# 48 gathered tokens in place of 64, one gathered row every 5.75 ticks, and four smaller edits around them

## The chip, the cores and the metric

The kernel runs on one core of one Trainium2 chip. The metric is the device time of one execution in microseconds (us). A profile of one execution goes with it: the span of the program, every instruction of the engines PE (matmul, with PEld for its weight loads), DVE, ACT, POOL and SP, the DMA queues, and the clock granted to PE.

## The reference

One decoder layer on 256 tokens of width 2048, in float32. Two token mixers are computed and merged (stage 1 below); the part that the change touches is the retrieval layer behind them. Each token has 8 heads; a head scores 128 + 128 keys, keeps 16 of each half and then the best 16 of their 256 sums, so that a token chooses 128 out of 16384 experts. An expert is one row of `expert_u` and one row of `expert_v`, 2048 numbers each.

```
q = h @ w_q                                   # 256 x 2048, 8 heads x 2 halves x 128
s1, s2 = q_half . sub_keys                    # 128 scores each
t1, i1 = top_k(s1, 16); t2, i2 = top_k(s2, 16)
ts, ti = top_k(t1[:, None] + t2[None, :], 16) # idx = i1 * 128 + i2
gate = softmax(ts)
act  = gelu(einsum('td,ted->te', h, expert_u[idx]))
y    = einsum('te,ted->td', gate * act, expert_v[idx])
out  = RMSNorm(x + y)
```

## The kernel before, in words

Everything is emitted in one program order; each engine runs its own instructions in that order, and waits for others by semaphores. Tokens lie along the free axis, so a weight block of 128 x 128 is the stationary operand and the tokens are the moving columns. For precision every weight block is split into a high part (ACT, `hi`, line 95) and a low part (DVE, `lo`, line 97), and the product uses high x (high and low tokens) and low x high tokens.

1. *Mixers* (to about 486 us of the profiled span).
2. *Queries* (about 486 to 585 us): 16 blocks of `w_q`; `query` scales each by the token's RMS factor `rstd2`; `scores` multiplies with the keys; the top-16 searches of tokens 128 to 255 run on DVE as side work (`topk_head`, `finish_topk(1)`). Those of tokens 0 to 127 are kept for stage 4.
3. *Dense loop* (about 585 to 1253 us): 128 steps, one for each block of 128 experts. `run_u` multiplies the block of `expert_u` with the first ND = 192 tokens: per step 16 pairs of matmuls, a wide one of 2 x ND = 384 columns (lines 796 and 800) and a narrow one of ND = 192 columns (lines 797 and 799), each with its own load of 128 x 128 weights. `evac` adds the two halves and stores the scores to a scratch array in DRAM, four blocks at a time (line 818). The last NG = 64 tokens are not in these matmuls: beside the loop, `u_job` gathers their chosen rows of `expert_u` (a gather fetches 128 rows of 8 KB, 1.05 MB) and DVE multiplies them with the token (line 674). A gather holds 8 experts of 16 tokens, so there are NG = 64 gathers, in groups of 16; `token_rows` makes for each group a tile `h2n` with the 16 tokens' vectors repeated in 8 partition blocks: PE transposes, ACT copies, and 7 copies from SBUF to SBUF on SP's DMA queue (line 750), the queue of the weights (`raw`). `v_job` gathers the 128 rows of `expert_v` of one token and multiplies them on PE (line 692, 8 matmul records). Gathers of both kinds go through `step`, with ROWS = 5 buffers. `work` is called four times a step; each call is a tick, and every PACE = 4.5 ticks `step` consumes one gathered row tile and issues a new gather on POOL.
4. *Tail* (from about 1253 us): the other `v_job`s, with one gather of elements (`se`, line 847) each: for one dense token, its 128 scores out of the scratch array. 16 elements make a group, `coefs` turns them into coefficients (DVE, ACT, DVE). `finish_topk(0)` comes here too: PE transposes of its result stand in PE's order (lines 630 and 631) between two `v_job`s.

`rest` are the gather jobs that the dense loop has not issued; the elements of the first group are spread over them.

Of the kernel before, what the change touches and what calls it, by code (L numbers as in the profile page):

```python
# [8 lines left out]
F32 = mybir.dt.float32  # L9
F32R = mybir.dt.float32r  # L10
F16 = mybir.dt.float16
U32 = mybir.dt.uint32
# [22 lines left out]
GT = 16  # L35
NG = 64
ND = T - NG
# [3 lines left out]
ROWS = 5  # L41
PACE = 4.5
FIRST_PACE = 6
LAST_PACE = 3
LEAD = 3
# [67 lines left out]
def block_kernel(ctx: ExitStack, tc: tile.TileContext,  # L113
# [9 lines left out]

    s_dram = nc.dram_tensor("s_scratch", (NK * P, ND), F32, kind="Internal").ap()

# [380 lines left out]
    idxS = gs.tile([P, ND], U32, name="idxS")  # L506
    gT = gs.tile([P, T], F32, name="gT")
    tpos = gs.tile([P, ND], F32, name="tpos")
    ident = gs.tile([P, P], F32, name="ident")
# [14 lines left out]
    run_b(ps, hhl, KC, whole=True)  # L524
    mean_square(accq, rstd2)
    mrg_stack.close()
    mix_stack.close()
# [73 lines left out]
    def finish_topk(tb):  # L601
# [12 lines left out]
        nd = min(ND, (tb + 1) * P) - tb * P  # L614
        if tb == TB - 1:
            pt = bank()
            for g in range(NG // GT):
# [16 lines left out]
        V.tensor_copy(idxV[:, ts], pt[:, 0:P])  # L634
        V.scalar_tensor_tensor(idxS[:, tb * P:tb * P + nd], pt[:, 0:nd], float(ND), tpos[:, tb * P:tb * P + nd],
                               op0=ALU.mult, op1=ALU.add)
# [97 lines left out]
    def token_rows(groups):  # L734

        for g in groups:
# [10 lines left out]

            def copies(g=g):
                for r in range(1, REP):
                    nc.sync.dma_start(h2n[g][r * GT:(r + 1) * GT], h2n[g][0:GT])  # L750

            later(copies, 2)

# [4 lines left out]
    def scores(n, qt):  # L758
# [5 lines left out]
        for tb in range(TB):  # L764
            S.copy(sc[tb], sp[:, tb * P:(tb + 1) * P])
        sc_keep[n] = sc
# [5 lines left out]
    def query(ps):  # L772
        qt = tkt.tile([P, T], F32, name="qt")
        V.tensor_mul(qt, ps[:, :T], rstd2)
        return qt
# [29 lines left out]
    def evac(i, ps):  # L805
# [11 lines left out]
        def store():  # L817
            nc.sync.dma_start(s_dram[(i + 1 - KB) * P:(i + 1) * P].rearrange("(k j) t -> j k t", j=P), es)

# [3 lines left out]
    for i in range(NK):  # L823
        if i == NK - 2:
            clock[2] = LAST_PACE
        ps = bank()
        run_u(ps)
        if i == 0:
            scores(15, qt)
            side.append(finish_topk(1))  # L830
        later(lambda i=i, ps=ps: evac(i, ps))
# [33 lines left out]
    left = GT  # L865
    for k, job in enumerate(rest):
        n = -(-left // (len(rest) - k)) if k >= 2 * len(rest) - GT else 1
        n = min(n, left)
# [72 lines left out]
```

## Time and profile before

| | us |
|---|---|
| median of 3 runs | 1833.71 (1832.51 to 1834.63) |
| the profiled execution | 1830.82 |
| its span | 1829.1 |
| busy in the span: PE / DVE / ACT / POOL | 1593.8 / 1062.4 / 727.0 / 594.0 |

The profiled execution's time is 1.7 us over its span and 2.9 us (0.16%) under the median. PE's busy time contains its pipeline latency, so how full PE is must be read from the starts of its matmuls, not from this sum.

### The profile page before, as it was taken

The numbers are of one execution on the slowest core, as the hardware profiler recorded it, in microseconds if no ns is written. First come the engines' busy times: TensorE is split into PE (matmuls) and PEld (weight loads), VectorE is DVE, ScalarE is ACT, GpSimd is POOL, SyncE is SP. The second block draws the span as 40 slices with busy tenths as digits, with TensorE's granted clock in tenths as the row PEclk, the third lists the DMA queues.
The fourth block names the chain that finished last, engine by engine and source line by source line (L and its number), as shares of the span: only waits on it lengthen the run. The fifth ranks groups of instructions, "written<-read, shape, count | busy, mean of one in ns | idle before, by whom it ended". The sixth has DMA issues, their size and how long they took to land.

```text
span 1829.1 us, 28362 instructions
## 1 busy us (share of the span) xinstructions
PE 1593.8 (87%) x10406; PEld 1190.9 (65%) x10406; DVE 1062.4 (58%) x2143; ACT 727.0 (40%) x1404; POOL 594.0 (32%) x607
## 2 busy tenths in 40 slices
PE   9999999999999899999999999997656666666665
PEld 7978888888899899899989999994111111111111
DVE  7887777777699789778767787776650000000000
ACT  7545555555544455555555555552010000000010
POOL 0130000000155311111112111113757777776762
PEclk9999999999999999999999999997767667667666
DMA  8546666566648799999999999998989999999997
GB/s 323 171 160 186 193 185 186 191 188 186 201 157 202 284 406 403 355 399 415 413 361 407 414 411 412 400 415 304 406 352 404 410 410 410 409 410 409 406 411 323
DMA packets 140012, 598.39 MB, mean 327 GB/s; under 512 B 21345, under 2 KB 37729, under 8 KB 98337
## 3 DMA queue, kind: packets, MB, share of 16 engines
q0 software_dynamic: 52496, 336.99, 45.9%
q1 hardware_dynamic: 87376, 259.60, 40.7%
q8 instruction: 81, 1.33, 0.3%
q14 instruction: 59, 0.48, 0.1%
HBM read 578.16 MB, written 14.68 MB: 324 GB/s over the span
## 4 chain that ended last, share of the span: by engine, by line
PE 41%; issue 30%; DMA 13%; POOL 11%; DVE 4%; SPq 0%; ACT 0%; POOLq 0%; DVEq 0%; ACTq 0%
PE acc L796 19%; DMA rows<-in_exp_v,idxV 9%; PE acc L797 8%; POOL rows L647 6%; POOL se L847 5%; PE y L692 3%; DMA raw<-in_exp_u 3%; PE acc L247 2%; PE acc L245 2%; PE acc L246 2%; DVE lo L97 1%; PE acc L800 1%; PE acc L251 1%; PE acc L252 1%; PE acc L250 1%
## 5 line engine op out<-in xcount | busy, mean ns | idle before, releaser
L97 DVE TENSOR_TENSOR lo<-raw,hi 128x512 fp32r<-128x512 f32 x854 | 577.3, 706 | 215.3 <-ACT hi L95 210.4
L95 ACT CAST hi<-raw 128x512 fp32r<-128x512 f32 x904 | 542.2, 619 | 357.7 <-PE acc L796 147.3
L796 PE MATMUL acc<-hhl,hi 128*128 128x384 f32 x1920 | 570.0, 364 | 5.7 <-ACT hi L95 5.7
L692 PE MATMUL y<-rows,cd 128*32 128x512 f32 x2048 | 380.2, 830 | 195.3 <-DMA rows<-in_exp_v,idxV 193.7
L797 PE MATMUL acc<-hhl,lo 128*128 128x192 f32 x1920 | 485.2, 253 | 3.8 <-DVE lo L97 3.7
L796 PEld LDWEIGHTS acc<-hhl,hi 128*128 128x128 f32 x1920 | 364.6, 190 | 38.7 <-ACT hi L95 28.0
L797 PEld LDWEIGHTS acc<-hhl,lo 128*128 128x128 f32 x1920 | 369.9, 193 | 6.5 <-DVE lo L97 6.5
L647 POOL DMA_INDIRECT rows<-in_exp_v,idxV x256 | 247.9, 968 | 359.7 <-DVE rows L674 228.5
L692 PEld LDWEIGHTS y<-rows,cd 128*32 128x32 f32 x2048 | 47.6, 125 | 474.3 <-DMA rows<-in_exp_v,idxV 431.8
L259 PE MATMUL acc<-hhl,hi 128*128 128x512 f32 x640 | 227.4, 398 | 1.6 <-ACT hi L95 1.6
L656 DVE TENSOR_TENSOR cx<-se,rstd 128x16 f32<-128x16 f32 x12 | 2.1, 175 | 363.6 <-DMA se<-s_scratch,idxS 363.6
L847 POOL DMA_INDIRECT se<-s_scratch,idxS x192 | 183.7, 957 | 70.1 <-issue 58.0
L261 PE MATMUL acc<-hhl,lo 128*128 128x256 f32 x600 | 169.3, 282 | 1.1 <-DVE lo L97 1.1
L657 ACT ACTIVATE cx<-cx 128x16 f32<-128x16 f32 x16 | 3.5, 216 | 407.5 <-DVE cx L656 407.5
L647 POOL DMA_INDIRECT rows<-in_exp_rows,idxU x64 | 68.9, 1077 | 267.0 <-DVE rows L674 195.8
L674 DVE SCALAR_TENSOR_TENSOR rows<-rows,h2n 128x2048 f32<-128x2048 f32 x64 | 146.1, 2283 | 0.0
L259 PEld LDWEIGHTS acc<-hhl,hi 128*128 128x128 f32 x640 | 119.7, 189 | 26.7 <-ACT hi L95 2.0
L541 POOL DMA_DIRECT2D keys<-in_keysT x1 | 0.6, 566 | 371.8 <-PE acc L305 371.8
L261 PEld LDWEIGHTS acc<-hhl,lo 128*128 128x128 f32 x600 | 114.0, 190 | 4.3 <-DVE lo L97 2.8
L245 PE MATMUL acc<-hhl,hi 128*128 128x256 f32 x384 | 110.3, 287 | 0.0
L247 PE MATMUL acc<-hhl,lo 128*128 128x256 f32 x384 | 109.0, 284 | 1.3 <-DVE lo L97 1.3
L246 PE MATMUL acc<-hhl,hi 128*128 128x256 f32 x384 | 108.6, 283 | 0.0
(191 smaller groups left out, 1738.3 us busy)
## 6 DMA issues: line engine op xcount, KB each, us to landing
raw<-in_exp_u SPq DMA_DIRECT2D x256, 512.0 KB, 9.7
raw<-in_w_in SPq DMA_DIRECT2D x96, 512.0 KB, 3.6
raw<-in_w_out SPq DMA_DIRECT2D x32, 512.0 KB, 4.0
raw<-in_w_q SPq DMA_DIRECT2D x32, 512.0 KB, 3.9
s_scratch<-es SPq DMA_DIRECT2D x32, 384.0 KB, 11.6
raw<-in_w_gproj SPq DMA_DIRECT2D x16, 512.0 KB, 4.6
raw<-in_w_v SPq DMA_DIRECT2D x15, 512.0 KB, 7.5
rows<-in_exp_v,idxV POOLq DMA_INDIRECT x256
```

The lines of the kernel that those rows point to most:

```text
L95: self.nc.scalar.copy(h, t)
L97: eng.tensor_sub(l, t, h.bitcast(F32))
L245: nc.tensor.matmul(ps, whi, ahi, start=first, stop=False)
L247: nc.tensor.matmul(ps, wlo, ahi, start=False, stop=last)
L259: nc.tensor.matmul(ps, whi, both, start=first, stop=last)
L261: nc.tensor.matmul(ps[:, :T], wlo, act[:, 0], start=False, stop=False)
L647: nc.gpsimd.indirect_dma_start(out=r, out_offset=None, in_=src, in_offset=bass.IndirectOffsetOnAxis(ap=idx, axis=0))
L674: V.scalar_tensor_tensor(r, r, 1.0, h2n[g], op0=ALU.mult, op1=ALU.mult, accum_out=act[g][:, n:n + 1])
L692: nc.tensor.matmul(y[q * GQ:(q + 1) * GQ], cd[:, m * GQ:(m + 1) * GQ], r[:, q * 512:(q + 1) * 512], start=(m == 0), stop=(m == GT - 1))
L796: nc.tensor.matmul(o2, whi[:, w], hhl[:, k, :, 0:ND], start=(k == 0), stop=False)
L797: nc.tensor.matmul(o1, wlo[:, w], hhl[:, k, 0, 0:ND], start=False, stop=False)
L847: nc.gpsimd.indirect_dma_start(out=se[t0][:, m:m + 1], out_offset=None, in_=flat, in_offset=bass.IndirectOffsetOnAxis(ap=idxS[:, t0 + m:t0 ...
```

## The change

NG goes from 64 to 48, so ND from 192 to 208: the dense matmuls have 416 and 208 columns, there are 48 gathers of `expert_u` in 3 groups, and 208 element gathers. The pace goes to 5.75 ticks and, for the last three steps, 2.5. The scratch array puts the four blocks of a store side by side, so a partition writes one piece of 3328 bytes where it wrote four of 768, and `finish_topk` computes the other index. The 7 copies of a token group are issued one at a time, some ticks apart. The query goes from PSUM to SBUF by an ACT copy without the factor, the factor is applied when the scores are copied, and for this the factor is brought into partitions (`rs2`) by two small matmuls. `finish_topk(1)` has 3.0 us of side-work credit more ahead of its matmuls.

```diff
--- before.py
+++ after.py
@@ -33,15 +33,15 @@
 AHEAD = 4
 WARM = 10
 GT = 16
-NG = 64
+NG = 48
 ND = T - NG
 REP = P // GT
 GQ = 32
 NQ = P // GQ
 ROWS = 5
-PACE = 4.5
+PACE = 5.75
 FIRST_PACE = 6
-LAST_PACE = 3
+LAST_PACE = 2.5
 LEAD = 3
 KB = 4
 HELD = 2
@@ -121,7 +121,7 @@
     def pool(stack, name, bufs=1, **kw):
         return stack.enter_context(tc.tile_pool(name=name, bufs=bufs, reuse_waits="tile", **kw))
 
-    s_dram = nc.dram_tensor("s_scratch", (NK * P, ND), F32, kind="Internal").ap()
+    s_dram = nc.dram_tensor("s_scratch", (NK // KB * P, KB * ND), F32, kind="Internal").ap()
 
     const = pool(ctx, "const")
     hp = pool(ctx, "hp")
@@ -505,6 +505,7 @@
     idxV = gs.tile([P, T], U32, name="idxV")
     idxS = gs.tile([P, ND], U32, name="idxS")
     gT = gs.tile([P, T], F32, name="gT")
+    rs2 = gs.tile([P, TB], F32, name="rs2")
     tpos = gs.tile([P, ND], F32, name="tpos")
     ident = gs.tile([P, P], F32, name="ident")
     fold = gs.tile([P, GT], F32, name="fold")
@@ -523,6 +524,10 @@
     ps = bank()
     run_b(ps, hhl, KC, whole=True)
     mean_square(accq, rstd2)
+    pt = bank()
+    for tb in range(TB):
+        nc.tensor.matmul(pt[:, 2 * tb:2 * tb + 2], rstd2[0:1, tb * P:(tb + 1) * P], one1, start=True, stop=True)
+    V.tensor_copy(rs2, pt[:, 0:4:2])
     mrg_stack.close()
     mix_stack.close()
     rp = pool(ctx, "rp", ROWS, side="right")
@@ -613,6 +618,7 @@
         ts = slice(tb * P, (tb + 1) * P)
         nd = min(ND, (tb + 1) * P) - tb * P
         if tb == TB - 1:
+            yield 3.0
             pt = bank()
             for g in range(NG // GT):
                 nc.tensor.matmul(pt[:, g * P:(g + 1) * P], wide[:, g].rearrange("p r t -> p (r t)"), ids,
@@ -632,7 +638,17 @@
         yield 0.1
         S.copy(gT[:, ts], pt[:, P:2 * P])
         V.tensor_copy(idxV[:, ts], pt[:, 0:P])
-        V.scalar_tensor_tensor(idxS[:, tb * P:tb * P + nd], pt[:, 0:nd], float(ND), tpos[:, tb * P:tb * P + nd],
+        at = tkt.tile([P, 2 * TOPK * TOPK], F32, name="oh", bufs=1)
+        at = at[:, 0:3 * P].rearrange("p (c t) -> p c t", c=3)
+        for c, (shift, mask) in enumerate(((9, NK - 1), (7, KB - 1), (0, NK - 1))):
+            part = tk.tile([P, P], U32, name="part")
+            V.tensor_scalar(part, idxV[:, ts], shift, mask, op0=ALU.logical_shift_right, op1=ALU.bitwise_and)
+            V.tensor_copy(at[:, c], part)
+        yield 1.0
+        V.scalar_tensor_tensor(at[:, 2], at[:, 0], float(P), at[:, 2], op0=ALU.mult, op1=ALU.add)
+        V.scalar_tensor_tensor(at[:, 1, 0:nd], at[:, 1, 0:nd], float(ND), tpos[:, tb * P:tb * P + nd],
+                               op0=ALU.mult, op1=ALU.add)
+        V.scalar_tensor_tensor(idxS[:, tb * P:tb * P + nd], at[:, 2, 0:nd], float(KB * ND), at[:, 1, 0:nd],
                                op0=ALU.mult, op1=ALU.add)
         yield 0.6
         if tb == TB - 1:
@@ -745,11 +761,12 @@
                 later(lambda g=g, q4=q4, pt=pt: S.copy(h2n[g][0:GT, q4 * 512:(q4 + 1) * 512], pt[0:GT]))
                 yield 3
 
-            def copies(g=g):
-                for r in range(1, REP):
-                    nc.sync.dma_start(h2n[g][r * GT:(r + 1) * GT], h2n[g][0:GT])
-
-            later(copies, 2)
+            def replicate(r, g=g):
+                nc.sync.dma_start(h2n[g][r * GT:(r + 1) * GT], h2n[g][0:GT])
+                if r < REP - 1:
+                    later(lambda: replicate(r + 1), 3 if g >= HELD else 1)
+
+            later(lambda: replicate(1), 2)
 
 
     sc_keep = {}
@@ -762,7 +779,7 @@
                              start=True, stop=True)
         sc = [tkt.tile([P, NK], F32, name=f"sc{tb}", bufs=16 if tb == 0 else 8) for tb in range(TB)]
         for tb in range(TB):
-            S.copy(sc[tb], sp[:, tb * P:(tb + 1) * P])
+            S.activation(sc[tb], sp[:, tb * P:(tb + 1) * P], AF.Copy, scale=rs2[:, tb:tb + 1])
         sc_keep[n] = sc
         if n % 2:
             pair = [sc_keep.pop(n - 1), sc_keep.pop(n)]
@@ -771,7 +788,7 @@
 
     def query(ps):
         qt = tkt.tile([P, T], F32, name="qt")
-        V.tensor_mul(qt, ps[:, :T], rstd2)
+        S.copy(qt, ps[:, :T])
         return qt
 
     qt = query(ps)
@@ -815,13 +832,13 @@
                 later(store, 6 if i < NK - 1 else 1)
 
         def store():
-            nc.sync.dma_start(s_dram[(i + 1 - KB) * P:(i + 1) * P].rearrange("(k j) t -> j k t", j=P), es)
+            nc.sync.dma_start(s_dram[i // KB * P:(i // KB + 1) * P], es.rearrange("j k t -> j (k t)"))
 
         S.copy(t, ps[:, ND:2 * ND])
         later(join)
 
     for i in range(NK):
-        if i == NK - 2:
+        if i == NK - 3:
             clock[2] = LAST_PACE
         ps = bank()
         run_u(ps)
@@ -864,6 +881,9 @@
         element()
     left = GT
     for k, job in enumerate(rest):
+        if k < len(rest) - GT:
+            jobs.append(job)
+            continue
         n = -(-left // (len(rest) - k)) if k >= 2 * len(rest) - GT else 1
         n = min(n, left)
         jobs.append(with_elements(job, n))
```

POOL at the start of the tail, in the order of the program: `rows` is a gather of `expert_v`, `se` an element gather. Before:

```order
L647 DMA rows<-in_exp_v,idxV 128x2048 x6
L847 DMA se<-s_scratch,idxS 128x1
L647 DMA rows<-in_exp_v,idxV 128x2048
L847 DMA se<-s_scratch,idxS 128x1
L647 DMA rows<-in_exp_v,idxV 128x2048
L847 DMA se<-s_scratch,idxS 128x1
```

Now:

```order
L663 DMA rows<-in_exp_v,idxV 128x2048 x18
L864 DMA se<-s_scratch,idxS 128x1 x4
L663 DMA rows<-in_exp_v,idxV 128x2048
L864 DMA se<-s_scratch,idxS 128x1 x3
L663 DMA rows<-in_exp_v,idxV 128x2048
L864 DMA se<-s_scratch,idxS 128x1 x3
L663 DMA rows<-in_exp_v,idxV 128x2048
L864 DMA se<-s_scratch,idxS 128x1 x3
L663 DMA rows<-in_exp_v,idxV 128x2048
L864 DMA se<-s_scratch,idxS 128x1 x3
L663 DMA rows<-in_exp_v,idxV 128x2048
L864 DMA se<-s_scratch,idxS 128x1
```

Before, each row gather has one element behind it (19 row gathers are left when the dense loop ends). Now 5 are left, and the 16 elements of the first group stand behind them as 4, 3, 3, 3, 3. Ahead of the first element there are 46 gathers of `expert_v` before and 44 now; behind it 210 and 212.

PE at the end of the first query block (`mean_square` is line 305). Before:

```order
L246 MATMUL acc<-hhl,hi 128x256
L247 MATMUL acc<-hhl,lo 128x256
L305 MATMUL acc<-accq_4465,ones 128x256
L245 MATMUL acc<-hhl,hi 128x256
L246 MATMUL acc<-hhl,hi 128x256
```

Now:

```order
L246 MATMUL acc<-hhl,hi 128x256
L247 MATMUL acc<-hhl,lo 128x256
L305 MATMUL acc<-accq_4465,ones 128x256
L529 MATMUL acc<-one_107,rstd_103 128x2 x2
L245 MATMUL acc<-hhl,hi 128x256
```

The two matmuls of line 529 read `rstd2`, which ACT and DVE make out of line 305's result; they stand between it and the next query block.

DVE at the end of the tail's top-16 search: `idf` holds the chosen indices, `ex` the gates, and the three rows with `cd` and `cx` are `coefs` of a group of elements. Before:

```order
L588 CAST abf<-ab 128x32
L655 MEMSET cd 128x512
L656 TENSOR_TENSOR cx<-se,rstd_103 128x16
L658 TENSOR_TENSOR cd<-cx,gT 128x16
L591 TENSOR_TENSOR oh<-abf,io_5562 128x512
L594 TENSOR_TENSOR oh<-oh,tif 128x512
L597 TENSOR_REDUCE sel<-oh 128x32
L598 SCALAR_TENSOR_TENSOR idf<-sel 128x16
L604 TENSOR_TENSOR ex<-cv 128x128
```

Now:

```order
L603 SCALAR_TENSOR_TENSOR idf<-sel 128x16
L609 TENSOR_TENSOR ex<-cv 128x128
L613 TENSOR_REDUCE sm<-ex 128x8
L614 RECIPROCAL sm<-sm 128x8
L615 TENSOR_TENSOR ex<-ex,sm 128x128
L671 MEMSET cd 128x512
L672 TENSOR_TENSOR cx<-se,rstd_103 128x16
L674 TENSOR_TENSOR cd<-cx,gT 128x16
L640 CAST idxV<-acc 128x128
```

The coefficients of the third group stood ahead of the last search's end; now they stand behind all that PE's two transposes read.

## Rows read from the trace of the kernel before

**Rows 1.** Windows: busy PE, PEld, DVE, ACT, POOL (instructions), PE clock, DMA share, GB/s
```profile
1050.00:1200.00 150.00, 150.00 (x1077) 137.95 (x1077) 116.65 (x182) 82.43 (x155) 27.82 (x26) 1.00 1.02 409
...
1400.00:1750.00 350.00, 228.29 (x1386) 41.84 (x1386) 15.88 (x54) 33.58 (x54) 256.37 (x272) 0.69 1.02 409
```

**Rows 2.** Timeline of PE, dense loop: start, us, engine, line, operation
```profile
1064.15 0.36 PE L800 MATMUL acc<-hhl,hi 128*128 128x384 f32 x1
...
1069.79 0.27 PE L799 MATMUL acc<-hhl,lo 128*128 128x192 f32 x1
1069.90 0.36 PE L800 MATMUL acc<-hhl,hi 128*128 128x384 f32 x1
...
1070.35 0.36 PE L796 MATMUL acc<-hhl,hi 128*128 128x384 f32 x1
...
1070.64 0.36 PE L796 MATMUL acc<-hhl,hi 128*128 128x384 f32 x1
...
1074.45 0.36 PE L800 MATMUL acc<-hhl,hi 128*128 128x384 f32 x1
```

**Rows 3.** Timeline of PE's weight loads in the same steps
```profile
1070.27 0.19 PEld L796 LDWEIGHTS acc<-hhl,hi 128*128 128x128 f32 x1
1070.38 0.19 PEld L797 LDWEIGHTS acc<-hhl,lo 128*128 128x128 f32 x1
```

**Rows 4.** Timeline of PE: matmuls that waited (idle before, and for whom)
```profile
606.83 2.07 PE L618 MATMUL acc<-idf,wide 128*128 128x128 f32 x8 [4.36 <-DVE idf L598]
...
776.76 0.69 PE L796 MATMUL acc<-hhl,hi 128*128 128x384 f32 x1 [2.69 <-ACT hi L95]
...
943.83 0.53 PE L796 MATMUL acc<-hhl,hi 128*128 128x384 f32 x1 [1.96 <-ACT hi L95]
```

**Rows 5.** Windows behind the first of these waits (columns as in rows 1)
```profile
606.00:613.00 7.00, 6.17 (x25) 6.17 (x26) 4.61 (x13) 1.82 (x5) 2.13 (x2) 0.51 0.26 94
613.00:620.00 7.00, 7.00 (x51) 7.00 (x50) 4.17 (x7) 3.94 (x7) 5.61 (x6) 1.00 0.77 280
```

**Rows 6.** Timelines of SP and ACT ahead of the wait at 776 us
```profile
753.97 7.60 SPq L750 DMA_DIRECT2D h2n<-h2n  x7
...
776.09 1.14 ACT L95 CAST hi<-raw 128x512 fp32r<-128x512 f32 x2 [8.33 <-DMA raw<-in_exp_u]
```

**Rows 7.** Timelines of PE and DVE at the first query block
```profile
486.24 0.47 PE L245 MATMUL acc<-hhl,hi 128*128 128x256 f32 x1
...
487.13 1.75 DVE L307 RECIPROCAL rstd<-rstd 128x256 f32<-128x256 f32 x1 [0.84 <-ACT rstd L306]
```

**Rows 8.** Waits of PE, 478 to 660 us (in total, times, longest); line 774
```profile
PE acc L797 <- DVE lo L97: 3.2, 4, 1.3
PE acc L761 <- DMA keys<-in_keysT: 1.5, 1, 1.5
...
L774 DVE TENSOR_TENSOR qt<-acc,rstd x16: 405/409/425, 490.7 to 590.7; 128x256 f32<-128x256 f32 x16
```

**Rows 9.** Timeline of POOL at the start of the tail
```profile
1262.68 0.95 POOL L847 DMA_INDIRECT se<-s_scratch,idxS  x1 [6.92 <-DMA s_scratch<-es]
1265.90 1.17 POOL L647 DMA_INDIRECT rows<-in_exp_v,idxV  x1 [2.27 <-issue]
...
1269.88 0.95 POOL L847 DMA_INDIRECT se<-s_scratch,idxS  x1 [0.30 <-issue]
1271.13 0.93 POOL L647 DMA_INDIRECT rows<-in_exp_v,idxV  x1 [0.30 <-issue]
```

**Rows 10.** Timelines of DVE, PE and POOL around the tail's transposes
```profile
1359.25 0.17 DVE L656 TENSOR_TENSOR cx<-se,rstd 128x16 f32<-128x16 f32 x1 [12.98 <-DMA se<-s_scratch,idxS]
...
1362.19 0.47 PE L630 MATMUL acc<-ident,idf 128*128 128x128 f32 x1 [9.95 <-DVE idf L598]
...
1366.26 0.94 POOL L647 DMA_INDIRECT rows<-in_exp_v,idxV  x1 [9.30 <-PE y L692]
```

**Rows 11.** Timeline of POOL: the last gather of the program
```profile
1809.91 0.94 POOL L647 DMA_INDIRECT rows<-in_exp_v,idxV  x1 [2.40 <-PE y L692]
```

## The prediction

> **What bounds the kernel now.** I read the windows first, to see which resource is full in which stage. In the dense loop and in the tail alike the DMA share is 1.02 at 409 GB/s [rows 1]. So DMA looks like the bound of both, and 16 fewer gathers of 1.05 MB like 41 us saved (16.8 MB at 409 GB/s). The share alone does not settle it, so I went to PE's timeline in the loop, to see whether PE ever waits there. From one end of a step (line 800) to the next it is 1069.90 - 1064.15 = 5.75 us where a `v_job` stands between, and 1074.45 - 1069.90 = 4.55 us where none does [rows 2]. Inside a step the pairs follow each other without a gap, 0.29 us from one wide matmul to the next [rows 2]; 4.55 / 16 = 0.284. DMA keeps pace, but PE's own work makes the step. PE had real waits in three places only: 4.36 us for the end of the top-16 search at 607 us, and 2.69 and 1.96 us for weights in the loop [rows 4].
>
> The tail is different. PE runs at a mean clock of 0.69 and is idle in between [rows 1]; the gathers set the time. From 1265.90 to the last at 1809.91 there are 209 of them after the first [rows 9, 11]. One stall is in that stretch: POOL idle for 9.30 us until PE freed a buffer [rows 10]. I count 8 of it as lost, since POOL has some idle time before any gather. (544.0 - 8) / 209 = 2.565 us each.
>
> **The change part by part.**
>
> *Wider matmuls, 16 x 128 = 2048 pairs.* What does a pair of 416 and 208 columns cost? Two narrow matmuls behind each other (line 799, then 800) start 0.11 us apart, and two loads of 128 x 128 weights also 0.11 us [rows 2, 3]. The narrow matmul has 192 columns, which at the full 2.4 GHz granted there, one per clock, take 0.080 us. So a narrow matmul does not set its own time: the next load, under which it runs, is longer. 208 columns take 0.087 us, still under 0.11, and cost nothing. The wide one takes 0.160 us of the pair (0.110 + 0.160 = 0.270, and 0.014 of overhead gives 0.284), and its 32 columns more take 13.3 ns. 2048 x 13.3 ns = **+27.2 us**. Bounds: 0, if loads alone made the pair (two of 0.142 us); and 48 / 576 of 0.284 = 23.7 ns, 48.5 us, if time went with columns. I take 13.3 because the 0.11 rows separate load from columns.
>
> The Trainium skill (TensorE: Matmul & The Clock Gate, section Back-to-back issue gap) gives an isolated warm matmul N / 2.4 + 2.5 ns. By that rule a pair would take 245 ns now and 265 ns then, +20 ns, +41 us in all. The trace has 284 and not 245 [rows 2], and the same section says that in a real stream the loads share in the spacing.
>
> *Fewer `v_job`s in the loop.* In the order, 38 stand there in place of 40. A step is 1.20 us longer with one [rows 2]: **-2.4**. One token group fewer is 32 small transposes fewer: between 0 and 32 x 0.11 = 3.5, I take **-2**. DVE's 16 multiplications of gathered rows that go were beside PE's work and count nothing.
>
> *The wait at 607 us.* It costs 4.36 us, and behind it the clock is at 0.51: 25 matmuls in 7 us where the next 7 hold 51 [rows 4, 5], so (51 - 25) / 51 x 7 = 3.6 us more. The change takes 16 x 0.41 us of query scaling from DVE [rows 8], and the order puts PE's matmuls one step (4.55 us) later. Either is enough for 4.36. The queries on ACT are hidden: in the loop it is busy 82 of 150 us [rows 1], and among the queries its copy stands behind one of scores that waits for PE anyway. I leave 0.5: **-7.5** (bounds -8 and 0).
>
> *Spread copies.* SP was held for 7.60 us by 7 copies, and the weights behind them came late: ACT waited 8.33 us for them, PE 2.69 [rows 4, 6]. The second group gave 1.96. I count 3.6 us of half clock for each as above: 2.69 + 1.96 + 7.2 = 11.8. Now one group is left in the loop, with loads between its copies; 1.1 us for one copy fits into the weights' lead of two steps. I leave 1: **-10.8** (bounds -11.8 and 0).
>
> *A new wait.* The matmuls of `rs2` stand on PE ahead of the next query block and need the reciprocal, which ends at 487.13 + 1.75 = 488.88; before, PE went on at 486.24 [rows 7]. With the matmuls themselves that is 2.9 us in which the whole query block queues behind them. Waits of 1.96 us and more were followed by half clock: another 0 to 3.6, I take 1.8. Against it, the first scores will no longer wait for their keys, 1.5, and the waits for `lo` (3.2 in all [rows 8]) shrink with DVE's queue, say by 1.7. Together **+1.5** (bounds 0 to 6.5).
>
> *The tail.* POOL takes 1.25 us from one issue to the next, row or element [rows 9]. Before, the first element went at 1262.68, and the last gather 547.2 us later [rows 9, 11]. Now the 16 elements share 5 gaps: 4 elements and a row, then 3 and a row four times over, so 16 elements and 4 rows lie between the first element's issue and that of the 49th gather of `expert_v`: 20 x 1.25 = 25.0 us. Then 207 gathers remain: 207 x 2.565 = 531.0. Together 556.0, so +8.8. Of this the burst is 11.6 (before, the fifth gather stood 1271.13 + 2 x 2.5 - 1262.68 = 13.4 behind the first element), the two more gathers are 5.1, and the stall's end gives back 8. The stall goes because DVE sat 12.98 us at `coefs`, waiting for a group's last element, with the end of the search queued behind it, and PE's transposes waited 9.95 for that [rows 10]; now `coefs` of the third group stands behind what the transposes need. The second group's blocks DVE instead, but some 15 gathers (38 us) ahead of the transposes, against about 29 us of search. The store with longer pieces may land sooner; POOL waited 6.92 for it [rows 9], so 0 to 6.9, I take 1. The new index arithmetic is on DVE, which has nothing else to do there; its results are read 50 gathers later. **+7.8** (bounds +2 and +17, the latter with the stall still there).
>
> *Sum.* 27.2 - 2.4 - 2 - 7.5 - 10.8 + 1.5 + 7.8 = +13.8 us on the profiled execution's 1830.8. That execution is 2.9 under the median, so against the median I expect 1833.7 + 13.8 = **1847 us**.
>
> **The rivals.**
>
> *A: both halves of the pair get longer,* 20 ns at 2.4 GHz for 48 columns: 41 us in place of 27.2, 1861 us. For it: nothing in the profile shows a narrow matmul with other than 192 columns between these loads. Against: the 0.11 us. Chance 0.09.
>
> *B, faster: weight loads alone pace the pair.* Then 416 columns run in the time of 384 and the loop only loses its waits: 1847.5 - 27.2 = 1820 us. For it: PEld is busy 138 of 150 us [rows 1], and a pair has two loads. Against: loads follow each other in 0.11 us when nothing is between [rows 3], so two need 0.22 of 0.284. It decides if the step without `v_job` stays under 4.63 us. Chance 0.12.
>
> *C: the burst of elements costs nothing,* because the row gathers in flight and the backlog of DMA cover 12 us: 1836 us, no change that can be told. For it: POOL waits for the store anyway, and up to four gathers are queued. Against: four gathers are 10 us, and they land while POOL waits. Chance 0.16.
>
> *D: a removed wait stays or comes back* (the one at 607 us, the copies, or PE at the transposes, 7 to 18 us): 1855 to 1865 us. Chance 0.13.
>
> **How the numbers follow.** The forecast has the remaining 0.50, with its own range of 1838 to 1856. Differences under 0.2% (3.7 us) can't be told from no change here. Faster by more: all of B, a third of C, little of the forecast: 0.20. Within: half of C and a little of the forecast: 0.12. Slower: 0.68. The range from 1828 to 1863 leaves out B and the ends of D.
>
> **What would show it.** Steps without a `v_job` of 4.76 us, from one line-817 matmul to the next (4.55: B; 4.87: A). No wait over 1 us on PE between 590 and 620 us and none for weights between 700 and 1250. A wait of about 2.9 us on PE near 486 us. In the tail, gathers about 5 us apart five times, then 2.5 to 2.6 us, and no idle stretch of POOL over 5 us at the transposes. The prediction is wrong if DMA and not PE makes the step, or if the tail's pace is not 2.56 us with 208 elements.

## The result and the profile after

The changed kernel takes 1854.48 us (median of 4 runs, 1854.45 to 1856.15), the kernel before 1833.11 beside it: a ratio of 1.0111, with a 95% interval of 1.0089 to 1.0132. It is 21 us slower; the forecast was 14 slower, at 1847, in a range of 1828 to 1863. The profiled execution took 1856.15 us with a span of 1854.5, 25.3 more than the span of before. All stretches below are of profiled executions.

First the windows that answer to [rows 1] (columns as there):

```profile
1050.00:1200.00 150.00, 150.00 (x1009) 138.99 (x1002) 106.69 (x167) 79.34 (x147) 20.86 (x20) 1.00 0.96 367
1400.00:1750.00 350.00, 227.20 (x1352) 39.08 (x1352) 14.11 (x48) 29.85 (x48) 255.14 (x271) 0.69 1.02 408
```

In this part of the loop DMA now has room (0.96, 367 GB/s); the tail is as it was. The loop moves less per us than before [rows 1] and still takes 13.3 us longer from its first matmul to its last step, so the 16 fewer gathers (16.8 MB) did not shorten it: PE's own work makes the step, as forecast. The timeline of PE's matmuls in the changed kernel, which answers to [rows 2]: the last matmul of three steps, and inside a step four wide ones with the narrow ones between them left out.

```profile
1041.90 0.37 PE L817 MATMUL acc<-hhl,hi 128*128 128x416 f32 x1
...
1046.70 0.37 PE L817 MATMUL acc<-hhl,hi 128*128 128x416 f32 x1
...
1051.66 0.37 PE L813 MATMUL acc<-hhl,hi 128*128 128x416 f32 x1
...
1051.96 0.36 PE L813 MATMUL acc<-hhl,hi 128*128 128x416 f32 x1
...
1052.26 0.36 PE L813 MATMUL acc<-hhl,hi 128*128 128x416 f32 x1
...
1052.67 0.36 PE L817 MATMUL acc<-hhl,hi 128*128 128x416 f32 x1
```

A step without a `v_job` takes 4.80 us (4.55 before), one with a `v_job` 5.97 (5.75), a pair 0.30. PE's waits are in these rows of its timeline:

```profile
487.92 0.98 PE L529 MATMUL acc<-one,rstd 1*128 1x2 f32 x4 [2.44 <-DVE rstd L307]
...
644.36 0.67 PE L813 MATMUL acc<-hhl,hi 128*128 128x416 f32 x1 [4.06 <-ACT hi L95]
...
802.23 0.46 PE L813 MATMUL acc<-hhl,hi 128*128 128x416 f32 x1 [1.54 <-ACT hi L95]
```

The first is the new wait for the reciprocal. The wait for the search's end at 607 us [rows 4] is gone, but one of 4.06 us for weights stands at 644, where [rows 4] had none so long. Of the waits for the copies one of 1.54 is left. Windows of the changed kernel behind the first wait, and at the second:

```profile
487.00:494.00 7.00, 6.08 (x28) 6.10 (x29) 3.08 (x7) 0.62 (x1) 3.13 (x3) 0.53 0.64 220
494.00:501.00 7.00, 7.00 (x60) 7.00 (x60) 1.97 (x2) 3.73 (x8) 2.57 (x2) 0.98 0.52 153
...
640.00:647.00 7.00, 2.88 (x11) 2.15 (x10) 2.66 (x3) 2.99 (x6) 0.00 (x0) 0.82 1.03 411
```

The granted clock is 0.53 behind the first wait: 28 matmuls in 7 us, then 60 at 0.98. At the wait of 644 us DMA is full (1.03). Last, POOL's timeline in the tail (answers to [rows 9 to 11]): the first element, the first two row gathers behind it, the gather after the transposes, and the last one.

```profile
1274.92 0.95 POOL L864 DMA_INDIRECT se<-s_scratch,idxS  x1 [2.84 <-DMA s_scratch<-es]
...
1280.03 0.94 POOL L663 DMA_INDIRECT rows<-in_exp_v,idxV  x1 [0.30 <-issue]
...
1285.02 0.94 POOL L663 DMA_INDIRECT rows<-in_exp_v,idxV  x1 [0.30 <-issue]
...
1358.83 1.05 POOL L663 DMA_INDIRECT rows<-in_exp_v,idxV  x1 [3.13 <-PE y L708]
...
1834.38 0.94 POOL L663 DMA_INDIRECT rows<-in_exp_v,idxV  x1 [0.70 <-PE y L708]
```

The burst is there (rows 5 us apart), and the stall of 9.30 us has become 3.13.

**Where the loop loses time.** The windows of a stage mix pace and waits, so I took the start of each step's last matmul, and from each distance to the next I took off the pace (4.80 us; 4.555 with 64 tokens) and 1.18 for a `v_job`; step 8, for example, is the distance from the end of step 8 to that of step 9. What is left is the loss: waits, half clock behind them, token transposes, and second `v_job`s in a step. In us, by steps:

| steps | before | 48 tokens alone | changed | 7 copies at once | gathers spread | 64 tokens, all other edits | same, three edits | and gathers spread |
|---|---|---|---|---|---|---|---|---|
| 0 to 9 | 14.4 | 14.0 | 12.3 | 14.7 | 5.6 | 13.0 | 14.6 | 7.0 |
| 10 to 29 | 2.8 | 1.6 | 0.5 | 0.5 | 1.5 | 0.5 | 0.5 | 6.8 |
| 30 to 59 | 8.7 | 6.6 | 6.8 | 8.6 | 6.5 | 12.9 | 9.7 | 11.6 |
| 60 to 79 | 9.0 | 0.4 | 0.2 | 0.2 | 0.2 | 8.2 | 9.1 | 8.6 |
| 80 to 127 | 1.7 | 5.6 | 4.7 | 4.7 | 4.7 | 1.6 | 1.6 | 1.7 |

The first column is the kernel before, the third the changed one; the others are experiments. Each column is one profiled execution. In the stretch of steps 30 to 59 the changed kernel and the four runs with the same matmuls and copies lie between 6.0 and 6.9 us, so a difference of 1 us there says little.

### The profile page after: what moved, and what is told of

Its sections match the earlier page's. It is cut to its first block, busy times and chain, and to the rows that moved or that the text cites. A ratio compares the mean times of both kernels' runs of the same rounds, so it can differ in the third digit from the quotient of the medians.

```text
span 1854.5 us, 28271 instructions
## 1 busy us (share of the span) xinstructions
PE 1618.4 (87%) x10374; PEld 1209.1 (65%) x10374; DVE 1031.9 (56%) x2108; ACT 736.0 (40%) x1416; POOL 590.5 (32%) x609
## 4 chain that ended last, share of the span: by engine, by line
PE 63%; DMA 12%; POOL 12%; issue 9%; DVE 3%; ACT 1%; SPq 0%; POOLq 0%; DVEq 0%; ACTq 0%
PE acc L813 19%; PE acc L259 13%; DMA rows<-in_exp_v,idxV 9%; PE acc L814 9%; POOL rows L663 6%; PE acc L261 6%; POOL se L864 5%; PE y L708 3%; PE acc L245 2%; PE acc L247 2%; PE acc L246 2%; DMA raw<-in_exp_u 2%; PE acc L817 1%; DVE lo L97 1%; PE acc L251 1%
## 5 line engine op out<-in xcount | busy, mean ns | idle before, releaser
L813 PE MATMUL acc<-hhl,hi 128*128 128x416 f32 x1920 | 591.4, 369 | 5.6 <-ACT hi L95 5.6
L814 PE MATMUL acc<-hhl,lo 128*128 128x208 f32 x1920 | 495.4, 258 | 4.2 <-DVE lo L97 3.6
L864 POOL DMA_INDIRECT se<-s_scratch,idxS x208 | 197.5, 950 | 71.3 <-issue 64.8
L663 POOL DMA_INDIRECT rows<-in_exp_rows,idxU x48 | 50.4, 1050 | 263.7 <-DVE rows L690 186.6
L690 DVE SCALAR_TENSOR_TENSOR rows<-rows,h2n 128x2048 f32<-128x2048 f32 x48 | 109.6, 2283 | 0.0
```

The lines of the kernel that those rows point to most:

```text
L663: nc.gpsimd.indirect_dma_start(out=r, out_offset=None, in_=src, in_offset=bass.IndirectOffsetOnAxis(ap=idx, axis=0))
L813: nc.tensor.matmul(o2, whi[:, w], hhl[:, k, :, 0:ND], start=(k == 0), stop=False)
L814: nc.tensor.matmul(o1, wlo[:, w], hhl[:, k, 0, 0:ND], start=False, stop=False)
L864: nc.gpsimd.indirect_dma_start(out=se[t0][:, m:m + 1], out_offset=None, in_=flat, in_offset=bass.IndirectOffsetOnAxis(ap=idxS[:, t0 + m:t0 ...
```

## The experiments

My theory was the prediction's sum with its sizes to be settled; the rivals named in each expectation stand against single terms of it. The first four runs take the change apart by size.

**All edits but the 48 tokens.**

```diff
-NG = 48
+NG = 64
-PACE = 5.75
+PACE = 4.5
-LAST_PACE = 2.5
+LAST_PACE = 3
-        if i == NK - 3:
+        if i == NK - 2:
```

> The changed kernel with the sizes of before (64 gathered tokens, 4.5 ticks, 3 for the last two steps); all other edits stay. Theory (the widths of the dense matmuls and the burst of 16 elements over 5 row gathers cost the time, the other edits together give some back): the step without a v_job goes back to 4.55 to 4.63 us, three row gathers stand ahead of the first element, 1812 to 1826 us. Rival (the other edits cost the time, the new wait ahead of the queries and the index arithmetic above all): over 1842 us.

Measured: 1834.5 us, 0.9999 of before (0.9980 to 1.0018). So the slowdown does belong to the 48 tokens, but the other edits were worth nothing here, where 8 to 22 us were expected. The table shows why in the loop: 36.2 us of losses for 36.7, the wait for the search gone and others in its place. In the tail the stall stayed, at the second transpose. PE's timeline of this run:

```profile
1346.83 0.48 PE L636 MATMUL acc<-ident,idf 128*128 128x128 f32 x1
1358.51 0.47 PE L637 MATMUL acc<-ident,ex 128*128 128x128 f32 x1 [11.21 <-DVE ex L615]
```

Here the third group's `coefs` still stands ahead of the gates `ex` in DVE's order and waits 11.83 us for its last element; DVE's timeline:

```profile
1355.53 0.17 DVE L672 TENSOR_TENSOR cx<-se,rstd 128x16 f32<-128x16 f32 x1 [11.83 <-DMA se<-s_scratch,idxS]
...
1356.07 0.29 DVE L609 TENSOR_TENSOR ex<-cv 128x128 f32<-128x128 f32 x1
```

One edit that the list of the change leaves out acts in this run: by the last hunk of the diff the first three of the 19 row gathers that are left get no element, so 49 gathers of `expert_v` and not 46 go out ahead of the first element. With 5 left it does nothing.

**The 48 tokens alone**, in the kernel before.

```diff
-NG = 64
+NG = 48
-PACE = 4.5
+PACE = 5.75
-LAST_PACE = 3
+LAST_PACE = 2.5
-        if i == NK - 2:
+        if i == NK - 3:
```

> The kernel before with the new sizes alone (48 gathered tokens, 5.75 ticks, 2.5 for the last three steps). Theory (widths and burst): steps without a v_job of 4.80 us, 1855 to 1868 us, as slow as the changed kernel or slower. Rival (the other edits cost): 1825 to 1840 us.

Measured: 1864.24 us, ratio 1.0149 (1.0126 to 1.0172), as expected. Between its span and the changed kernel's lie 9.4 us: the other edits make the loop 5.8 shorter (687.0 to 681.2, of which 3.8 are losses in the table) and the stretch from the first element to the last gather 7.1 (566.6 to 559.5, with a gap of 10.89 between row gathers in the former); the loop's later start takes 3.7 back. The stall is in this run too, because `coefs` again stands ahead of `ex`; PE's timeline:

```profile
1395.63 0.47 PE L631 MATMUL acc<-ident,ex 128*128 128x128 f32 x1 [12.20 <-DVE ex L610]
```

So neither the new count of elements nor the other edits alone take the stall away; both together do. The two parts of the change are not independent: the other edits are worth nothing with 64 tokens and 9.8 us (1864.24 - 1854.48) with 48.

**Which half of the pair the columns cost.** First the narrow matmuls back to 192 columns (16 tokens lose the product with the low part of the weights), then the wide ones back to 2 x 192 in 15 of 16 pairs (16 tokens lose most of theirs).

```diff
+NSUB = 192
...
-                    nc.tensor.matmul(o1, wlo[:, w], hhl[:, k, 0, 0:ND], start=False, stop=False)
+                    nc.tensor.matmul(ps[:, 0:NSUB], wlo[:, w], hhl[:, k, 0, 0:NSUB], start=False, stop=False)
...
-                    nc.tensor.matmul(o1, wlo[:, w], hhl[:, k, 0, 0:ND], start=False, stop=False)
+                    nc.tensor.matmul(ps[:, 0:NSUB], wlo[:, w], hhl[:, k, 0, 0:NSUB], start=False, stop=False)
```

> The changed kernel, but the narrow matmul of each pair runs over 192 columns; 16 tokens go without the low part of their weights. Theory (the narrow matmul is hidden under a weight load of 0.11 us): the step without a v_job stays at 4.77 to 4.82 us, time 1850 to 1857 us. Rival A of the prediction (both halves cost their columns, 6.7 ns a pair for this one): 4.69 us, 1840 to 1845 us.

```diff
-                    nc.tensor.matmul(o2, whi[:, w], hhl[:, k, :, 0:ND], start=(k == 0), stop=False)
+                    n = ND if k == 0 else NSUB
+                    nc.tensor.matmul(o2[:, :, 0:n], whi[:, w], hhl[:, k, :, 0:n], start=(k == 0), stop=False)
...
-                    nc.tensor.matmul(o2, whi[:, w], hhl[:, k, :, 0:ND], start=False, stop=True)
+                    nc.tensor.matmul(o2[:, :, 0:NSUB], whi[:, w], hhl[:, k, :, 0:NSUB], start=False, stop=True)
```

> The changed kernel, but the wide matmul of each pair runs over 2 x 192 columns in 15 of 16 pairs; 16 tokens lack these products. The narrow one keeps 208. Theory (the wide half alone costs): the step without a v_job is 4.55 to 4.63 us, time 1823 to 1833 us. Rival A (13.3 of 20 ns are the wide half): 4.66 to 4.70 us, 1837 to 1843 us. Rival B (weight loads pace the pair): no change from 4.80 us.

Narrow ones back: 1861.93 us, a step of 4.85, longer and not shorter; rival A, to which this run should have given 4.69, is out, but the run also came out above the theory's own figures. Wide ones back: 1829.68 us and 4.60 a step, inside the expectation. PE's timelines, first with narrow 192:

```profile
1051.67 0.38 PE L814 MATMUL acc<-hhl,hi 128*128 128x416 f32 x1
1051.89 0.25 PE L815 MATMUL acc<-hhl,lo 128*128 128x192 f32 x1
1051.97 0.38 PE L814 MATMUL acc<-hhl,hi 128*128 128x416 f32 x1
```

and with wide 384:

```profile
1052.06 0.35 PE L815 MATMUL acc<-hhl,hi 128*128 128x384 f32 x1
1052.25 0.26 PE L816 MATMUL acc<-hhl,lo 128*128 128x208 f32 x1
1052.35 0.35 PE L815 MATMUL acc<-hhl,hi 128*128 128x384 f32 x1
```

From a narrow matmul to the wide one behind it are 0.08 us with 192 columns and 0.10 with 208, but what is saved there is lost on the way from the wide one to the next narrow one (0.22 with narrow 192; 0.21, as median, in the changed kernel). Over a whole pair the wide matmul decides: (4.80 - 4.60) / 15 = 13.3 ns for 32 columns. The narrow one's 16 columns are worth 4.60 - 4.555 = 0.045 us a step, of which 0.013 is the one pair left wide.

The weight loads show where the 32 columns go. First the kernel before, behind the loads of [rows 3], then the changed one:

```profile
1070.55 0.19 PEld L796 LDWEIGHTS acc<-hhl,hi 128*128 128x128 f32 x1
```

```profile
1050.67 0.19 PEld L813 LDWEIGHTS acc<-hhl,hi 128*128 128x128 f32 x1
1050.78 0.19 PEld L814 LDWEIGHTS acc<-hhl,lo 128*128 128x128 f32 x1
1050.97 0.19 PEld L813 LDWEIGHTS acc<-hhl,hi 128*128 128x128 f32 x1
```

From the high load to the low one, under which the narrow matmul runs, are 0.11 us in both. From the low load to the next high one are 0.17 before and 0.19 now (medians over the loop: 176 and 190 ns; 178 with wide 384, 194 with narrow 192). So all of the growth lies under the wide matmul.

The Trainium skill (TensorE: Matmul & The Clock Gate, section LDWEIGHTS) prices a load by its columns, P / 1.2 ns; by that an estimate for 128 columns is 107 ns. The trace agrees with it for the high load (0.11 us).

**The copies at once again**, in the changed kernel.

```diff
                 if r < REP - 1:
-                    later(lambda: replicate(r + 1), 3 if g >= HELD else 1)
+                    replicate(r + 1)
```

> The changed kernel with the seven copies of a token group issued at once again, as before the change; nothing else differs. Theory (spreading gives next to nothing: the run with 48 tokens alone lost 6.6 us over its pace in the steps 30 to 60, the changed kernel 6.8): the time and the steps 30 to 60 stay within 2.5 us of the changed kernel, and PE waits for weights once, two to four steps earlier than at 802 us. Rival (the prediction's term, 10.8 us for two groups, so 5.4 for the one that is left): about 5.4 us longer than the changed kernel, all of it in the steps 30 to 60.

Measured: 1859.76 us in one run, 5.3 over the changed kernel's median and not within the 2.5 that were expected; the spans differ by 3.6. The place decides between the theory and its rival. In its own stretch (steps 30 to 59) the run loses 8.6 us where the changed kernel loses 6.8: spreading is worth 1.8 us there, and not 5.4. Another 2.4 us of the difference lie in steps 0 to 9, at the wait near 644 us (step 8 loses 8.5 in place of 6.9). PE's wait for the third group's copies is in its timeline:

```profile
791.39 0.55 PE L813 MATMUL acc<-hhl,hi 128*128 128x416 f32 x1 [3.85 <-ACT hi L95]
```

It is longer than the 1.54 us at 802 us; but there two waits for `lo` of 1.6 us together come with it, so spreading has split the wait more than removed it.

**The factor's matmuls later**, in the changed kernel: behind the second query block, ahead of the first scores (with a tile `onec` of ones of their own).

```diff
-    pt = bank()
-    for tb in range(TB):
-        nc.tensor.matmul(pt[:, 2 * tb:2 * tb + 2], rstd2[0:1, tb * P:(tb + 1) * P], one1, start=True, stop=True)
-    V.tensor_copy(rs2, pt[:, 0:4:2])
+    nc.gpsimd.memset(onec, 1.0)
...
         run_b(ps, hhl, KC, TK_CREDIT, whole=True)
+        if n == 1:
+            pr = bank()
+            for tb in range(TB):
+                nc.tensor.matmul(pr[:, 2 * tb:2 * tb + 2], rstd2[0:1, tb * P:(tb + 1) * P], onec, start=True, stop=True)
+            V.tensor_copy(rs2, pr[:, 0:4:2])
```

> The changed kernel with the two small matmuls that bring the factor into partitions moved behind the second query block, just ahead of the first scores, so that no query block queues behind the reciprocal. Theory (this wait and the half clock behind it are the 3.0 us by which the dense loop begins later): no PE wait and no half clock near 487 us, and the dense loop begins 2.4 to 4 us earlier than in the changed kernel, at 584.3 to 585.9. If it lasts, the first element gather of the tail goes out that much earlier too. Rival (the time is given back where PE next runs out of weights or of the search's end): the loop begins earlier, and its first ten steps take as much longer, so that the first element gather is within 1 us of the changed kernel's.

Measured: 1852.21 us in one run; no wait and no half clock near 487 us; the dense loop begins at 583.9 in place of 588.3, and the first element goes out at 1270.65 in place of 1274.92. It lasts; the rival is out. One pair flatters it: over all runs the loop begins at 585.6 to 588.3 (mean 587.1 of 8) with this wait, and at 583.9 to 585.3 (mean 584.7 of 5) without, so it is worth 2.4 us. A wait for the keys of 1.0 us comes back.

**At most two gathers a tick**, in the changed kernel.

```diff
+FILL = 2
...
-        while jobs and len(fetched) < ROWS - 1:
+        for _ in range(min(len(jobs), ROWS - 1 - len(fetched), FILL)):
```

> The changed kernel with at most two gathers issued at a tick, so that the first five gathers of expert_u go out as 2, 2 and 1, some 7 us apart, and not five within 6.5 us. Theory (the wait that the change removes at 607 us comes back at 644 us, because the burst of five gathers takes the DMA queues while PE now runs on without a rest): the wait for weights near 644 us and its half clock shrink from 6.9 us over the pace in step 8 to under 2.5, and the time falls by 4 to 7 us against the changed kernel. Rival (weights and gathers together ask for more than DMA moves in these steps, whatever the order): the wait only moves by some steps, and the first 15 steps together stay within 2 us.

Measured: 1851.28 us, a loss of 6.8 and 0.9 us in steps 8 and 9, and 686.6 us from the loop's start to the first element, all much as in the changed kernel. But the run tests nothing: POOL still issued five gathers, one right behind the other, from 613.81 to 618.93. Written further apart, they went out as before; the next run gives POOL something to wait for.

**The first gathers really spread**, in the changed kernel: two indices at once, each further one copied by DVE ahead of its gather.

```diff
+    depth = [1.75]
...
+        depth[0] = min(depth[0] + 0.25, ROWS - 1)
-        while jobs and len(fetched) < ROWS - 1:
+        while jobs and len(fetched) < int(depth[0]):
...
-            V.tensor_copy(idxU, sel)
+            V.tensor_copy(idxA, sel[:, 0])
+            V.tensor_copy(idxU[:, 1:], sel[:, 1:])
+            V.tensor_copy(idxU[:, 0, 0:2], sel[:, 0, 0:2])
...
-        return lambda: fetch(exp_rows, idxU[:, g, n:n + 1]), consume
+        def issue():
+            if g == 0 and n > 1:
+                V.tensor_copy(idxU[:, g, n:n + 1], idxA[:, n:n + 1])
+            return fetch(exp_rows, idxU[:, g, n:n + 1])
+
+        return issue, consume
```

> The changed kernel with the first gathers of expert_u spread in time: only two indices are written at once, each further one of the first group (for these alone) is copied by DVE just ahead of its gather, so that POOL waits for it, and the number of gathers on their way grows from two to four over eight ticks of the pace. The run with two gathers a tick did not test this: there POOL ran ahead and still issued five gathers 1.25 us apart. Theory (the burst of five gathers beside the weights is what PE waits for near 644 us): the third gather goes out 10 us or more behind the second, and the loss of step 8, 6.9 us over the pace, falls under 2, so that the first element gather of the tail goes out 4 to 7 us earlier behind the start of the dense loop than the 686.6 us of the changed kernel. Rival (DMA is short over a longer stretch, so that the wait only moves): a wait for weights of the same size comes 5 to 20 steps later, and these 686.6 us stay within 2.

Measured: 1848.27 us in one run, and 680.5 us in place of 686.6 from the loop's start to the first element. POOL's timeline:

```profile
617.48 0.96 POOL L668 DMA_INDIRECT rows<-in_exp_rows,idxU  x1 [0.30 <-issue]
632.66 1.14 POOL L668 DMA_INDIRECT rows<-in_exp_rows,idxU  x1 [14.22 <-DVE idxU L705]
```

and all of PE's waits from 478 to 660 us (in total, times, longest):

```profile
PE acc L532 <- DVE rstd L309: 2.4, 1, 2.4
PE acc L824 <- DVE lo L97: 2.1, 4, 0.8
PE acc L824 <- POOL lo L97: 0.4, 2, 0.2
```

The wait for weights is gone, 1.0 us of it comes back in steps 10 to 29 (the table's column for this run), and the granted clock stays full from 494 us up to the tail. So the wait at 644 us is the five gathers: 5 x 1.05 MB stand beside the steps' own 1.05 MB each.

The Trainium skill (DMA: Bandwidth & Descriptors, section Specifications) gives the fabric a ceiling of 435 GB/s and a core's share of the HBM about 358. With one core at work the trace has 411 GB/s at the wait and 408 in the tail, above the second figure and near the first.

**One element to a row**, in the changed kernel: 11 of the first group's 16 element gathers are left out, and their scores are taken as zero.

```diff
+        if t0 != P or m in (0, 4, 7, 10, 13):
+            nc.gpsimd.indirect_dma_start(out=se[t0][:, m:m + 1], out_offset=None, in_=flat,
```

> The changed kernel without 11 of the 16 element gathers of the first group (their scores are taken as zero), so that one element stands behind each of the five row gathers that are left. Theory (the burst costs POOL's issue time, 1.25 us for each element, since no more than four row gathers are queued ahead): from the first element to the last gather of expert_v 11 to 14 us less than the 559.5 us of the changed kernel. Rival C of the prediction (the backlog of DMA covers the burst): within 3 us of 559.5.

Measured: 1843.69 us in one run. From the first element (1273.12) to the last gather (1823.44) it is 550.3 us in place of 559.5: 9.2 less, short of the expected 11 to 14 and far from rival C. To the 50th gather of `expert_v` it is 13.9 us in place of 27.6, so the 13.7 are POOL's issue time (11 x 1.25), but the 206 gathers behind it take 4.6 us longer.

**Two stalls taken out at 64 tokens**: all edits with 64 tokens, as in the first run, the factor's matmuls later, and the tail's side-work credit raised so that the third `coefs` falls behind the search's end.

```diff
-V_CREDIT = 1.5
+V_CREDIT = 1.7
```

> The changed kernel with 64 gathered tokens, the pace of before, the factor's two matmuls behind the second query block, and 1.7 in place of 1.5 us of side-work credit in the tail, which puts the coefficients of the third group behind the end of the last search. Theory (with 64 tokens the other edits were worth nothing because the wait for the reciprocal came in and the stall of 11.57 us at PE's second transpose stayed): no gap between row gathers over 6 us at 1340 to 1380 us, the last gather of expert_v 546 to 549 us behind the first 16 us of the tail's steady part as before less 6 to 9 us, and a time of 1820 to 1829 us, faster than before by 0.3 to 0.8%. Rival (what the stall costs is taken back, since DMA has a backlog to work off in the meantime and PE waits for rows behind it anyway): the gap is gone and the last gather stands within 2 us of the run with 64 tokens, 555.4 us behind the dense loop's end; 1830 to 1836 us, no change that can be told from before.

Measured: 1824.02 us, 0.9949 of before (0.9931 to 0.9967): faster than both kernels. The last gather stands 547.9 us behind the loop's end, as expected (555.4 in the first run); from the first element to it are 535.6 us against 543.9, and the gap of 11.57 us between row gathers at the transposes is gone. One of 6.53 us at 1323 (5.59 in the first run) lies outside the stretch that was named. PE's timeline:

```profile
1336.98 0.48 PE L634 MATMUL acc<-ident,idf 128*128 128x128 f32 x1 [3.46 <-DVE idf L601]
1338.41 0.47 PE L635 MATMUL acc<-ident,ex 128*128 128x128 f32 x1 [0.95 <-DVE ex L613]
```

**And the gathers spread as well**: the edit of the first gathers on top of these three.

> The run with 64 tokens and three edits (factor's matmuls later, more side-work credit) with the first gathers spread in time as well, as in the run that took the loss of step 8 away. Theory (that wait is the same with 64 tokens, 7.1 and 0.75 us over the pace in steps 8 and 9): the first ten steps lose 6 to 9 us less, and the time is 1815 to 1819.5 us, faster than before by 0.75 to 1.0%. Rival (with 64 tokens DMA is full from there to the end of the loop, so that gathers that are put off are missed later): the wait for weights behind the copies near 790 us grows from 6.6 us, or the tail begins with fewer gathers done, and the time stays at 1821 to 1826 us.

Measured: 1825.36 us, 0.9941 (0.9918 to 0.9964). The rival holds. The first ten steps lose 7.0 us in place of 14.6, but steps 10 to 29 lose 6.8 in place of 0.5 and steps 30 to 59 1.9 more: 35.7 in all for 35.5. Windows from 660 to 740 us, first without the edit:

```profile
660.00:740.00 80.00, 80.00 (x568) 80.00 (x568) 74.63 (x112) 47.35 (x88) 13.62 (x12) 1.00 1.02 402
```

then with it:

```profile
660.00:740.00 80.00, 76.25 (x525) 73.81 (x523) 69.26 (x112) 41.03 (x82) 14.68 (x13) 1.00 1.02 408
```

With 64 tokens DMA is full in both, and with the edit PE has small waits there: gathers that were put off are missed later. With 48 tokens the same edit gains 6 us, although DMA is as full in the same window (here in the run of the changed kernel with the first gathers spread):

```profile
660.00:740.00 80.00, 79.58 (x532) 78.60 (x531) 70.31 (x114) 42.80 (x84) 15.05 (x13) 1.00 1.02 413
```

So a full window alone does not decide. What differs is the load further on: 0.96 and 367 GB/s from 1050 to 1200 us with 48 tokens, 1.02 and 409 before [rows 1]. That this room lets DMA catch up fits both runs; no run varied it alone.

## Why the prediction was nearly right

The sum was made in spans, +13.8, and the spans differ by 25.3 (the medians by 21). By its own steps:

| term | forecast | measured |
|---|---|---|
| wider matmuls | +27.2 | +31.1 |
| fewer `v_job`s in the loop | -2.4 | -2.1 |
| a token group fewer, spread copies | -12.8 | -10.7 |
| the wait at 607 us | -7.5 | -2.1 |
| other losses in the loop | 0 | -2.9 |
| the new wait, up to the loop's start | +1.5 | +3.0 |
| loop's end to the last gather | +7.8 | +8.2 |
| behind the last gather | 0 | +0.9 |

The measured sizes: 127 x (4.80 - 4.555) for the first; rows of the table of losses for the third and fourth (steps 30 to 79 and 0 to 9); steps 10 to 29 and 80 to 109 for the fifth; the second is what the loop's +13.3 leaves, with the second `v_job`s of the last steps and the loop's first step in it. All rows but one came out dearer than forecast, by 14.5 us together; the 2.9 us of other losses went the other way, and nobody had forecast them: luck. That the result lies in the range owes as much to the range's width as to the sum.

**Wider matmuls.** The step was to be 4.76 and is 4.80. The mechanism held: the run with wide 384 gives back 13.3 ns a pair, the very figure of the forecast. What failed is "cost nothing" for the narrow ones, by some 2 ns a pair. One reading behind it was wrong as well: the 0.11 us from line 799 to line 800 [rows 2] do not lie between two narrow matmuls. They run from a narrow one to a wide one in the step's last pair, whose order is turned round. In the other pairs the wide matmul starts 0.09 us behind a narrow one of 192 columns (median), so matmul starts show no floor of 0.11; the loads do, and they carry the argument.

**The wait at 607 us.** This is the largest miss: the 7.5 us were booked as gone, and 2.1 came. The wait did go, and steps 0 to 7 lose 5.4 us in place of 10.8; of the 2.1 that are missing there, 1.5 are short waits for `lo` in steps 2 to 4. Behind it PE ran into the weights at 644 us, which five gathers had made late: steps 8 and 9 lost 3.6 us before, and the changed kernel loses 6.9. The step of the forecast that failed is that PE had "real waits in three places only". The kernel before was short of weights here too:

```profile
641.67 0.44 PE L796 MATMUL acc<-hhl,hi 128*128 128x384 f32 x1 [1.05 <-ACT hi L95]
```

That the burst makes this wait is shown by the spread gathers. That it grew because PE no longer rests at 607 is only argued. It fits the order of events, and steps 8 and 9 lose more without the rest at either size (64 tokens: 3.6 with it, 6.4 without; 48 tokens: 5.3 and 6.9), but the other edits differ in these pairs too. It is rival D in the one place: 5.4 us of the term did not come.

**Copies.** The sum of -12.8 nearly came out, but not for the reason of the heading "Spread copies". The run with 48 tokens alone, copies at once, has the same losses behind step 30 as the changed kernel (7.0 and 7.0 us in steps 30 to 79), and with 64 tokens spreading left 21.1 and 18.8 for 17.7. What counts is that one group of copies is gone (steps 60 to 79: 9.0 to 0.2); spreading the other is worth 1.8. The sign "none for weights between 700 and 1250" failed: a wait of 1.54 us is left at 802.

**The new wait.** 2.44 us and the half clock behind it: +3.0 in this profile, 2.4 over several runs, within the bounds of 0 to 6.5. The forecast's remark that waits of 1.96 us and more were followed by half clock does not hold for every run (last section).

**The tail.** The burst's 25.0 us (25.1 measured) and the vanished stall were right; two sizes were off and cancel, which is luck. The first element came 4.1 us earlier behind the loop's end, where 1 was taken for the store; no run isolates why. From it to the last gather it is +12.2 us and not +8.8: the stretch of the transposes, gathers 70 to 100, gave 6.5 us (85.4 to 78.9) for the 8, and other gathers took the rest. The 207 gathers behind the burst took 534.4 us and not 531.0.

**The rivals.** B (step under 4.63) and A (4.87) are ruled out by the step of 4.80; C by the run with one element to a row. The result lies where the forecast's own range and rival D meet.

## What to carry to other kernels

A wait that is removed frees its engine to reach the next shortage sooner: before booking the gain, ask what is late next, and whether a burst (here five gathers at once) waits just behind it. A small wait in the profile of before is a hint of where that will be. Before spreading a burst, ask what room its resource has later: the same edit gave 6 us where DMA stood at 0.96 late in the loop, and nothing where it stood at 1.02. To hold back a queue that runs ahead, give it something to wait for; to write its instructions later did nothing here. And run the parts of a change both alone and without each other: here the same edits were worth 0 or 9.8 us, by the size that they stood beside.

## What was not expected of the hardware

A narrower matmul made the stream slower: pairs of 416 and 192 columns take 303 ns, those of 416 and 208 columns 300 (4.85 and 4.80 us a step); pairs of 384 and 208 take 287, those of 384 and 192 285. Why the first of these is the wrong way round stays open. The half clock behind one and the same wait cost different amounts in different runs: with the same program up to there, the dense loop began at 585.6 us in one run and at 588.3 in another, so that a single run can misjudge such a wait by 2 us and more. In three of the eight runs with this wait of 2.44 us the granted clock stayed full behind it, and the loop began at 585.6 to 586.0; in the five with half clock behind it, at 587.4 to 588.3.
